# Two transformer blocks on one core: a list scheduler that plans in three passes and ranks ready instructions by deadlines

## The chip, the cores and the metric

The kernel runs on one core of a Trainium2 chip. The metric is the device time of one execution in microseconds (us), from the first to the last instruction and what lies around them; smaller is better. The engines are named as the profile names them: PE (TensorE, the matrix engine; PEld is its weight loading), DVE (VectorE), ACT (ScalarE), POOL (GpSimd) and SP (SyncE, which here only starts DMAs). On-chip memory is SBUF; PE writes its results to PSUM.

## The reference, cut to what matters

Two blocks follow each other, each of two layers and a final norm; 256 tokens of width 1024, fp32. Each layer is a gated feed-forward step of width 2816, a mixing step, and another feed-forward step. The mixing differs: block 1 has neighbourhood attention and gated linear attention (GLA), block 2 has forgetting attention, dilated attention with rotary positions, and HGRN2.

```python
def swiglu(h, w_gate, w_up, w_down):
    return (jax.nn.silu(h @ w_gate) * (h @ w_up)) @ w_down
def hybrid_layer(x, ...):                       # block 1, layer l
    x = x + 0.5 * swiglu(rmsnorm(x, ffn1_norm), ffn1_wg, ffn1_wu, ffn1_wd)
    proj = rmsnorm(x, mix_norm) @ w_in
    na_o = rmsnorm(neighbourhood_attention(na_q, na_k, na_v, na_rpb), na_gain)
    gla_o = rmsnorm(o_fwd + o_bwd, gla_gain) * silu(g_r)   # GLA in both directions
    x = x + concatenate([na_o, gla_o]) @ w_out
    x = x + 0.5 * swiglu(rmsnorm(x, ffn2_norm), ffn2_wg, ffn2_wu, ffn2_wd)
def gla_chunked(q, k, v, g, include_diag):      # one chunk
    b = cumsum(g)
    decay = exp(where(mask, b[:, None] - b[None], -inf))
    a = einsum('td,sd,tsd->ts', q, k, decay)
    ...
def _mixing(h, ...):                            # block 2
    proj = h @ w_in
    oa = _fox_attention(fq, fk, fv, cumsum(log_sigmoid(ff + fox_b)))
    ob = _dilated_attention(_partial_rope(dq), _partial_rope(dk), dv)
    oc = _hgrn2(hq, hf, hi, hg, lb, hgrn_norm)
    return concatenate([oa, ob, oc]) @ w_out
```

## The kernel before, in words

**The matrix products.** Every weight comes from memory as fp32 tiles of 128x1024, 128x704 or 128x768 (`raw`, four buffers, 512 KB each for the largest), started on SP's queue in a fixed sequence. ACT copies a tile to a rounded form (`whi<-raw`), DVE subtracts (`wlo<-raw,whi`), so that a weight is the sum of a high and a low part; activations are kept as a high and a low half side by side (`xhl`, 512 columns). For each 128x128 block of a weight PE multiplies the high part by both halves (128x512) and the low part by the high half (128x256) into the same PSUM bank. This pair is called a block pair below. Banks `acc` and `o` hold features by tokens, `wi` tokens by features. ACT and DVE add the halves (`b<-acc`, `t<-acc,b`) and scale by the norm (`t<-t,rb`, `proj<-t,rb`). A weight tile is wanted by ACT, DVE and PE in the same sequence everywhere.

**The mixing steps.** There are four, called the first to the fourth mixer; the first two belong to block 1. In them the products with `w_in` and `w_out` go on while DVE, ACT and POOL compute the mixing on small tiles. In block 1, DVE scans the gates in two pairs (`C<-g`, four scans in each row), POOL subtracts them (`kq<-C`, function `differences` in `Mixer1.gla`), ACT takes the exponential (`kq<-kq`), DVE multiplies (`kq<-kq,proj`), and PE makes one level of the decay matrix from it (`psA<-kq`, eight levels), which DVE merges (`mg<-mk,psA`). Beside that PE computes attention scores (`psS`), DVE the softmax (`S`, `mx`, `sm`), PE turns them (`psP`). SP moves 16 slabs of values within SBUF in each of these layers (`proj<-proj`, function `slabs`). In block 2 the same chain is called `X<-C`, `X`, `psA<-X`; DVE also turns the dilated heads (`rope<-proj,cs`, `proj<-rope`) before PE transposes them (`psT<-ident,proj`), and computes the forget gate (`fz`, ACT's `ls_e`, `lf`), on which the scores `psS<-tri,lf` rest; ACT takes their exponential (`E`).

**What sets the order.** Nothing is issued while the program is written down: `Program.record` makes an `Op` of each call, with the tiles it uses, its dependencies and an estimated duration (`cost`, and `occ` for PE in `record`, lines 300 to 313). A `Driver` writes the stages down as tasks and jobs; `op.n` is an operation's place in that text. `Program.order` (lines 359 to 452) is a list scheduler: for each of the engines it looks at the operations whose dependencies are placed and whose tile buffers open, and takes the one that could begin first in its model, on a tie the one with the smaller `op.n`:

```python
est = max(op.ready, at, free[e])
k = (est, op.n)
if best[e] is None or k < best[e][0]:
    best[e] = (k, op)
```

The model has one time per engine, a hop of 0.06 between engines, and lets DVE operations with two inputs in SBUF and POOL's exclude each other (`op.port`). `issue` (line 454) then issues all operations in that sequence, so each engine works through a fixed queue in order, and every instruction of the profile has the line 460 (504 in the changed kernel). Buffers of a tile name are handed out in the sequence of the text.

Of the kernel before, what the change touches and what calls it, by code (L numbers as in the profile page):

```python
# [37 lines left out]
def lay_blocks(w, order):  # L38

    b = np.stack([w[f * P:(f + 1) * P, g * P:(g + 1) * P] for g, f in order])  # L40
    return np.ascontiguousarray(b.reshape(-1, 8, P, P).transpose(0, 2, 1, 3)).reshape(-1, P, 8 * P)
# [57 lines left out]
class View:  # L99


    __slots__ = ("tile", "shadow", "chain", "made")

    def __init__(self, tile, shadow, chain=()):
        self.tile, self.shadow, self.chain, self.made = tile, shadow, chain, None
# [80 lines left out]


class Op:
    __slots__ = ("n", "engine", "calls", "occ", "lat", "deps", "after", "wait", "ready", "start", "tiles", "mode", "port")

    def __init__(self, n, engine):
        self.n, self.engine, self.calls, self.occ, self.lat = n, engine, [], 0.0, 0.0
        self.deps, self.after, self.wait, self.ready, self.start = {}, [], 0, 0.0, None
        self.tiles, self.mode, self.port = {}, None, False


class Recorder:
# [7 lines left out]
def free_size(x):  # L205
    n = 1
    for k in x.shape[1:]:
        n *= k
    return n


class Program:
# [61 lines left out]
    def record(self, engine, name, args, kw):  # L274
# [8 lines left out]
        if pe and self.unit is not None:  # L283
            op = self.unit
        else:
            op = Op(len(self.ops), engine)
# [10 lines left out]
        n = max([free_size(x) for x in views] or [1])  # L297
        if pe:
            out, l, r = args[:3]
            if name == "transpose":  # L300
                rows, cols, m = r.shape[0], out.shape[-1], l.shape[0]
                occ = 0.109
                mode = (128, 128)
            else:
                rows, cols, m = l.shape[0], l.shape[-1], free_size(r)
                mode = (128 if rows > 64 else 64, 128 if cols > 64 else 64)
                if r.dtype == F32R:
                    occ = max(m / 2400.0 + (0.02 if m > 256 else 0.0085), 0.109)
                else:
                    occ = 2 * max(m / 1200.0, cols / 1200.0, 0.025) / (2 if mode == (64, 64) else 1) + 0.005  # L310
            if op.mode is not None and op.mode != mode:
                occ += 0.09
            op.mode = mode
            op.occ += occ
            op.lat = self.DRAIN
        else:
            op.occ, op.lat = self.cost(engine, name, args, kw, writes[0] if writes else None, n)
            srcs = [x for x in views if not any(x is w for w in writes) and free_size(x) > 1]
            op.port = name in ("tensor_tensor", "scalar_tensor_tensor") and len(srcs) > 1 and \
                not any(x.tile.bank for x in srcs)  # L320
# [4 lines left out]
        for x in views:  # L325
            t = x.tile
            if op not in t.__dict__.setdefault("seen", set()):
# [3 lines left out]
                if t.index is None:  # L331
                    line = self.tags.setdefault(t.tag, [])
# [24 lines left out]
        t.marks = keep  # L357

    def order(self):
        ops = self.ops  # L360
        for op in ops:
            op.deps.pop(op, None)
            op.wait = len(op.deps)
            for d in op.deps:
                d.after.append(op)
        engines = ("tensor", "scalar", "vector", "gpsimd", "sync")
        free = dict.fromkeys(engines, 0.0)
        avail = {e: [] for e in engines}
# [4 lines left out]
        dma, mode, out = 0.0, None, []  # L373
        port = {"vector": 0.0, "gpsimd": 0.0}

        def opening(op):

            at, need = 0.0, {}
            for t in op.tiles:
                if t.opened:  # L380
                    continue
                s = state[t.tag]
                k = need.get(t.tag, 0)
                if t.index != s[0] + k or s[1] + k >= t.bufs:
                    return None
                if s[0] + k >= t.bufs:
                    at = max(at, s[2][k] + self.HOP)
                need[t.tag] = k + 1
            return at

        best = dict.fromkeys(engines)
        stale = set(engines)
        while len(out) < len(ops):
            for e in stale:
                best[e] = None
                for op in avail[e]:
                    at = opening(op)
                    if at is None:
                        continue
                    est = max(op.ready, at, free[e])  # L400
                    k = (est, op.n)
                    if best[e] is None or k < best[e][0]:
                        best[e] = (k, op)
            stale = set()
            e = min((x for x in engines if best[x]), key=lambda x: best[x][0])
            (start, _), op = best[e]
            avail[e].remove(op)
            stale.add(e)
            if op.port:
                start = max(start, port["gpsimd" if e == "vector" else "vector"])  # L410
# [3 lines left out]
            if e == "tensor":  # L414
                mode = op.mode
            free[e] = start + op.occ + extra
            end = free[e] + op.lat
            if op.calls[0][0] == "dma_start":
# [3 lines left out]
                end = dma + 1.3  # L422
# [17 lines left out]
            for o in op.after:  # L440
# [7 lines left out]
                if not o.wait:  # L448
                    avail[o.engine].append(o)
                    stale.add(o.engine)  # L450
        self.ordered, self.free = out, free
        return out

    def issue(self):
        for op in self.order():
# [1473 lines left out]
```

## Time and profile before

| | |
|---|---|
| time, median of 3 runs | 2033.12 us (2032.52 to 2034.95) |
| the profiled execution, its own time | 2034.24 us |
| its span, first to last instruction | 2032.5 us |
| mean granted PE clock | 0.994 |
| matmuls on PE | 12604 |
| instructions in all | 33794 |

The profile shows one execution. A row of a group names engine, operation, what is written and what is read (buffer numbers left out), how often, and idle time of the engine just before, with the engine and tile that ended it. The chain of waits follows the instruction that ended last back to the first. A stretch's row gives how long each engine was busy within a window of the execution and which share of full clock PE was granted. The feed-forward steps take most of the time; the mixers lie at about 200 to 340, 690 to 840, 1180 to 1340 and 1690 to 1850 us.

### The profile page before, as it was taken

Reading aid. Unit: us, or ns where it says so; the run is one execution under the profiler, and the core shown is the slowest. Engines: PE = TensorE matmul, PEld = TensorE weight load, DVE = VectorE, ACT = ScalarE, POOL = GpSimd, SP = SyncE. Lnnn points to the kernel's source line nnn. Section 1 sums busy time; section 2 is a strip of 40 time slices with the busy share of each in tenths; the row PEclk is TensorE's granted clock in tenths of the full one; section 3 lists DMA queues with packets and bytes.
Section 4 is the critical chain, followed back from the end, with each engine's and each line's share of the span. In section 5 each row is a group of like instructions: output and inputs, shape, how many; then the busy total and the mean of one; then the engine's idle time right before and its main releaser. Section 6 shows DMA issues by size and latency. Waiting matters only on the chain.

```text
span 2032.5 us, 33794 instructions
## 1 busy us (share of the span) xinstructions
PE 1991.9 (98%) x12604; PEld 1745.3 (86%) x12604; DVE 1566.1 (77%) x2405; ACT 1203.5 (59%) x2073; POOL 485.3 (24%) x502
## 2 busy tenths in 40 slices
PE   8999999999999999999999998999999999899997
PEld 7888888888888888888888897888888888788886
DVE  7876888876887698887698678788768867878874
ACT  6654666654665566665566465766546656576653
POOL 3341604331221151221232004122112210412210
PEclk9999999999999999999999999999999999999999
DMA  7655446565555544555566553465555555346652
GB/s 232 196 195 177 151 137 198 192 192 191 181 191 191 161 152 147 192 192 188 176 201 188 193 169 104 128 197 190 190 186 188 187 194 162 122 125 197 191 193 94
DMA packets 104629, 357.35 MB, mean 176 GB/s; under 512 B 13460, under 2 KB 15012, under 8 KB 104464
## 3 DMA queue, kind: packets, MB, share of 16 engines
q1 hardware_dynamic: 101040, 352.20, 54.3%
q0 software_dynamic: 3136, 2.47, 0.5%
q8 instruction: 99, 1.62, 0.3%
q14 instruction: 66, 0.54, 0.1%
q10 hardware_dynamic: 288, 0.52, 0.1%
HBM read 351.98 MB, written 1.51 MB: 174 GB/s over the span
## 4 chain that ended last, share of the span: by engine, by line
PE 84%; DVE 9%; ACT 3%; POOL 2%; issue 1%; DMA 1%; SPq 0%; DVEq 0%; ACTq 0%; POOLq 0%
PE acc L460 51%; PE o L460 27%; DVE wlo L460 3%; PE wi L460 2%; POOL kq L460 1%; ACT whi L460 1%; DVE x L460 1%; PE psO L460 1%; DVE proj L460 1%; DVE xhl L460 1%; DVE X L460 1%; DVE t L460 1%; DVE kq L460 1%; PE psN L460 0%; PE psS L460 0%
## 5 line engine op out<-in xcount | busy, mean ns | idle before, releaser
L460 PE MATMUL acc<-xhl,whi 128*128 128x512 f32 x3328 | 1057.4, 398 | 6.8 <-DVE xhl L460 2.4
L460 DVE TENSOR_TENSOR wlo<-raw,whi 128x1024 fp32r<-128x1024 f32 (+3 forms) x682 | 827.6, 1214 | 187.7 <-ACT whi L460 174.5
L460 ACT ACTIVATE whi<-raw 128x1024 fp32r<-128x1024 f32 (+3 forms) x682 | 704.8, 1034 | 346.3 <-PE o L460 200.1
L460 PEld LDWEIGHTS acc<-xhl,wlo 128*128 128x128 f32 x3328 | 627.1, 188 | 146.9 <-DVE wlo L460 0.4
L460 PE MATMUL acc<-xhl,wlo 128*128 128x256 f32 x3328 | 659.2, 279 | 0.0
L460 PEld LDWEIGHTS acc<-xhl,whi 128*128 128x128 f32 x3328 | 510.4, 189 | 13.8 <-DVE xhl L460 3.7
L460 PE MATMUL o<-hT,whi 128*128 128x512 f32 x1408 | 442.2, 395 | 0.0
L460 POOL TENSOR_TENSOR s<-s,rb 128x256 f32<-128x256 f32 x176 | 215.6, 1225 | 668.0 <-ACT s L460 663.9
L460 ACT ACTIVATE b<-acc 128x256 f32<-128x256 f32 x416 | 158.1, 382 | 332.9 <-PE acc L460 332.5
L460 PEld LDWEIGHTS o<-hT,wlo 128*128 128x128 f32 x1408 | 264.5, 188 | 62.5
L460 DVE TENSOR_TENSOR t<-acc,b 128x256 f32<-128x256 f32 x416 | 174.5, 421 | 139.9 <-ACT b L460 139.8
L460 PE MATMUL o<-hT,wlo 128*128 128x256 f32 x1408 | 276.6, 278 | 0.0
L460 PEld LDWEIGHTS o<-hT,whi 128*128 128x128 f32 x1408 | 214.3, 189 | 0.0
L460 POOL TENSOR_TENSOR sqs<-sqs,sq 128x256 f32<-128x256 f32 x88 | 77.0, 878 | 491.5 <-ACT sq L460 490.9
L460 PE MATMUL wi<-whi,xhl 128*128 128x352 f32 (+2 forms) x448 | 118.8, 335 | 0.8 <-ACT X L460 0.8
L460 DVE SCALAR_TENSOR_TENSOR x<-o,x 128x256 f32<-128x256 f32 x192 | 78.0, 420 | 40.5 <-PE o L460 38.3
L460 DVE TENSOR_TENSOR t<-t,rb 128x256 f32<-128x256 f32 x200 | 86.2, 431 | 5.7
L460 DVE TENSOR_TENSOR t<-t,s 128x256 f32<-128x256 f32 x176 | 75.9, 431 | 18.0 <-POOL s L460 1.2
L460 ACT ACTIVATE s<-t 128x256 f32<-128x256 f32 x176 | 73.4, 417 | 24.7 <-DVE t L460 15.7
L460 DVE TENSOR_TENSOR hT<-t,hT 128x256 fp32r<-128x256 f32 x176 | 84.0, 477 | 0.1
L460 ACT ACTIVATE hT<-t 128x256 fp32r<-128x256 f32 x176 | 73.3, 417 | 18.2 <-DVE t L460 8.3
L460 PEld LDWEIGHTS wi<-whi,xhl 128*128 128x128 f32 x448 | 80.4, 188 | 2.2 <-ACT X L460 1.1
(192 smaller groups left out, 1390.4 us busy)
## 6 DMA issues: line engine op xcount, KB each, us to landing
raw<-in_gu_dram SPq DMA_DIRECT2D x350, 512.0 KB, 3.4
raw<-in_wd_dram SPq DMA_DIRECT2D x176, 512.0 KB, 3.4
raw<-in_win_dram SPq DMA_DIRECT2D x64, 512.0 KB, 3.7
raw<-in_wo_dram SPq DMA_DIRECT2D x32, 512.0 KB, 3.7
raw<-in_win_dram SPq DMA_DIRECT2D x24, 384.0 KB, 3.0
raw<-in_win_dram SPq DMA_DIRECT2D x24, 352.0 KB, 3.0
raw<-in_win_dram SPq DMA_DIRECT2D x8, 388.0 KB, 3.0
proj<-proj SPq DMA_DIRECT2D x32, 64.0 KB, 2.1
```

The costliest lines, as they stand in the source:

```text
L460: getattr(e, name)(*args, **kw)
```

## The change

Operations get a rank, which is `op.n` at first. `order` now runs the same list scheduler (`forward`) three times and keeps the sequence whose modelled end is the earliest. Between two passes `backward` goes through the sequence from its end and gives each operation the latest start at which its dependents, and those that reuse its buffers, are still in time; only PE's operations are also chained one behind the other. That latest start is the operation's rank in the next pass. Among the operations that could begin within 0.001 us of the earliest one, an engine takes the one with the smallest rank, then the smallest `op.n`. Apart from that, PE's modelled cost of small matmuls depends on whether the one before in the same operation has the same shape. No instruction's own work is changed.

```diff
--- before.py
+++ after.py
@@ -186,12 +186,12 @@
 
 
 class Op:
-    __slots__ = ("n", "engine", "calls", "occ", "lat", "deps", "after", "wait", "ready", "start", "tiles", "mode", "port")
+    __slots__ = ("n", "engine", "calls", "occ", "lat", "deps", "after", "wait", "ready", "start", "tiles", "mode", "port", "rank", "late", "left")
 
     def __init__(self, n, engine):
         self.n, self.engine, self.calls, self.occ, self.lat = n, engine, [], 0.0, 0.0
         self.deps, self.after, self.wait, self.ready, self.start = {}, [], 0, 0.0, None
-        self.tiles, self.mode, self.port = {}, None, False
+        self.tiles, self.mode, self.port, self.rank = {}, None, False, n
 
 
 class Recorder:
@@ -304,10 +304,12 @@
             else:
                 rows, cols, m = l.shape[0], l.shape[-1], free_size(r)
                 mode = (128 if rows > 64 else 64, 128 if cols > 64 else 64)
+                side_by_side = op.mode == mode
                 if r.dtype == F32R:
                     occ = max(m / 2400.0 + (0.02 if m > 256 else 0.0085), 0.109)
                 else:
-                    occ = 2 * max(m / 1200.0, cols / 1200.0, 0.025) / (2 if mode == (64, 64) else 1) + 0.005
+                    side = {(128, 128): 1, (128, 64): 2, (64, 128): 2, (64, 64): 4}[mode] if side_by_side else 1
+                    occ = 2 * max(m / 1200.0 / side, cols / 1200.0 if side == 1 else 0.019, 0.019) + 0.005
             if op.mode is not None and op.mode != mode:
                 occ += 0.09
             op.mode = mode
@@ -357,12 +359,54 @@
         t.marks = keep
 
     def order(self):
+
+        for op in self.ops:
+            op.deps.pop(op, None)
+            for d in op.deps:
+                d.after.append(op)
+        for line in self.tags.values():
+            for t in line:
+                t.uses = t.left
+        best = None
+        for k in range(self.PASSES):
+            end, out = self.forward()
+            if best is None or end < best[0]:
+                best = end, out
+            if k < self.PASSES - 1:
+                self.backward(out)
+        self.ordered = best[1]
+        return self.ordered
+
+    PASSES = 3
+
+    def backward(self, out):
+
+        last = max(op.start + op.occ for op in out)
+        front, frees = {}, {}
+        for line in self.tags.values():
+            for t in line:
+                t.needed = last
+        for op in reversed(out):
+            late = front.get(op.engine, last) if op.engine == "tensor" else last
+            for o in op.after:
+                late = min(late, o.rank - (0.0 if o.engine == op.engine else op.lat + self.HOP))
+            for t in op.tiles:
+                late = min(late, t.needed)
+            op.rank = late - op.occ
+            front[op.engine] = op.rank
+            for t in op.tiles:
+
+                if t.index >= t.bufs:
+                    p = self.tags[t.tag][t.index - t.bufs]
+                    p.needed = min(p.needed, op.rank - self.HOP)
+
+    def forward(self):
         ops = self.ops
         for op in ops:
-            op.deps.pop(op, None)
-            op.wait = len(op.deps)
-            for d in op.deps:
-                d.after.append(op)
+            op.wait, op.ready = len(op.deps), 0.0
+        for line in self.tags.values():
+            for t in line:
+                t.left, t.opened, t.end = t.uses, False, 0.0
         engines = ("tensor", "scalar", "vector", "gpsimd", "sync")
         free = dict.fromkeys(engines, 0.0)
         avail = {e: [] for e in engines}
@@ -392,18 +436,18 @@
         stale = set(engines)
         while len(out) < len(ops):
             for e in stale:
-                best[e] = None
+                best[e], can = None, []
                 for op in avail[e]:
                     at = opening(op)
-                    if at is None:
-                        continue
-                    est = max(op.ready, at, free[e])
-                    k = (est, op.n)
-                    if best[e] is None or k < best[e][0]:
-                        best[e] = (k, op)
+                    if at is not None:
+                        can.append((max(op.ready, at, free[e]), op.rank, op.n, op))
+                if can:
+                    first = min(can)[0] + 0.001
+                    k = min((x for x in can if x[0] <= first), key=lambda x: x[1:3])
+                    best[e] = k[:3], k[3]
             stale = set()
             e = min((x for x in engines if best[x]), key=lambda x: best[x][0])
-            (start, _), op = best[e]
+            (start, *_), op = best[e]
             avail[e].remove(op)
             stale.add(e)
             if op.port:
@@ -448,8 +492,8 @@
                 if not o.wait:
                     avail[o.engine].append(o)
                     stale.add(o.engine)
-        self.ordered, self.free = out, free
-        return out
+        self.free = free
+        return max(free.values()), out
 
     def issue(self):
         for op in self.order():
```

The feed-forward steps keep PE's sequence. The first place where the order moves is the first mixer (the second moves alike). On SP's queue, around the 16 slab moves, before and now:

```order
L460 DMA raw<-in_win_dram 128x1024 x4
L460 DMA raw<-in_win_dram 128x704 x4
L460 DMA raw<-in_win_dram 128x1024 x6
L460 DMA proj<-proj 32x512 x16
L460 DMA raw<-in_win_dram 128x1024 x2
L460 DMA raw<-in_win_dram 128x704 x4
```

```order
L504 DMA raw<-in_win_dram 128x1024 x6
L504 DMA proj<-proj 32x512 x2
L504 DMA raw<-in_win_dram 128x1024
L504 DMA proj<-proj 32x512 x5
L504 DMA raw<-in_win_dram 128x1024
L504 DMA proj<-proj 32x512 x7
L504 DMA raw<-in_win_dram 128x704
L504 DMA proj<-proj 32x512 x2
L504 DMA raw<-in_win_dram 128x704 x3
```

The slab moves stood in one piece ahead of the next weights; now three weight tiles go in between them.

On DVE, at the scans of the same mixer (`g` is the gate, `C` its running sum), before and now:

```order
L460 SCALAR_TENSOR_TENSOR g<-psZ,ls_e 128x512
L460 SCALAR_TENSOR_TENSOR C<-g,zero 128x128 x4
L460 SCALAR_TENSOR_TENSOR g<-psZ,ls_e 128x512
L460 TENSOR_TENSOR t<-acc,b 128x256
L460 SCALAR_TENSOR_TENSOR C<-g,zero 128x128 x4
L460 SCALAR_TENSOR_TENSOR proj<-t,rb 128x256
L460 TENSOR_TENSOR wlo<-raw,whi 128x704
L460 TENSOR_TENSOR t<-acc,b 128x256
L460 TENSOR_TENSOR wlo<-raw,whi 128x704
L460 SCALAR_TENSOR_TENSOR proj<-t,rb 128x256
```

```order
L504 SCALAR_TENSOR_TENSOR g<-psZ,ls_e 128x512
L504 SCALAR_TENSOR_TENSOR C<-g,zero 128x128 x4
L504 SCALAR_TENSOR_TENSOR g<-psZ,ls_e 128x512
L504 TENSOR_TENSOR t<-acc,b 128x256
L504 TENSOR_TENSOR wlo<-raw,whi 128x704
L504 SCALAR_TENSOR_TENSOR proj<-t,rb 128x256
L504 TENSOR_TENSOR t<-acc,b 128x256
L504 TENSOR_TENSOR wlo<-raw,whi 128x704
L504 SCALAR_TENSOR_TENSOR proj<-t,rb 128x256
L504 SCALAR_TENSOR_TENSOR C<-g,zero 128x128 x4
```

The second row of scans stood right behind the second gate and one addition; now two weight splits of 704, two scalings and an addition more go ahead of it.

The second place is the third mixer (the fourth moves alike in this part). On PE, where the scores of the forgetting attention follow the last levels of HGRN2, before and now:

```order
L460 MATMUL psA<-X 64x32 x16
L460 MATMUL psA<-X,proj 64x32 x16
L460 MATMUL psS<-tri,lf 128x128 x2
L460 MATMUL psS<-M_11173,identr 128x2x128
L460 MATMUL psS<-tri,lf 128x128 x4
L460 MATMUL psS<-M_11173,identr 128x2x128
L460 MATMUL psS<-tri,lf 128x128 x2
L460 MATMUL psS<-proj 128x256 x4
L460 MATMUL psP<-ident,E 128x128 x8
```

```order
L504 MATMUL psA<-X 64x32 x16
L504 MATMUL psA<-X,proj 64x32 x16
L504 MATMUL wi<-whi,xhl 128x384
L504 MATMUL wi<-wlo,xhl 128x384
L504 MATMUL wi<-whi,xhl 128x384 x2
L504 MATMUL wi<-wlo,xhl 128x384
L504 MATMUL wi<-whi,xhl 128x384 x2
L504 MATMUL wi<-wlo,xhl 128x384
L504 MATMUL wi<-whi,xhl 128x384 x2
L504 MATMUL wi<-wlo,xhl 128x384
L504 MATMUL wi<-whi,xhl 128x384
L504 MATMUL psS<-tri,lf 128x128 x2
```

The scores stood directly behind the levels; now a whole weight tile's products (`wi`, nine rows) come first. Another such tile moved ahead of the levels.

On DVE, at the rotary step of the third mixer, before and now:

```order
L460 TENSOR_TENSOR wlo<-raw,whi 128x1024
L460 SCALAR_TENSOR_TENSOR C<-proj,zero 128x128
L460 COPY_PREDICATED mg<-mk_11171,psA 128x256
L460 TENSOR_TENSOR wlo<-raw,whi 128x1024 x2
L460 TENSOR_SCALAR proj<-wi,rstd 128x384
L460 TENSOR_TENSOR rope<-proj,cs 128x256 x2
L460 TENSOR_TENSOR X<-X,proj 128x16x32
L460 TENSOR_TENSOR proj<-rope 128x2x8x8
```

```order
L504 TENSOR_TENSOR wlo<-raw,whi 128x1024
L504 TENSOR_TENSOR fz<-proj,fb 128x4
L504 TENSOR_TENSOR wlo<-raw,whi 128x1024
L504 TENSOR_SCALAR proj<-wi,rstd 128x384
L504 TENSOR_TENSOR wlo<-raw,whi 128x1024
L504 TENSOR_TENSOR rope<-proj,cs 128x256 x2
L504 TENSOR_TENSOR X<-X,proj 128x16x32
L504 TENSOR_TENSOR proj<-rope 128x2x8x8
```

Two weight splits stood between the last scans and `rope`; now there are three.

## Rows read from the trace of the kernel before

**Rows 1.** Page: busy time of each engine (share of the span), instructions; the chain, by engine.

```profile
PE 1991.9 (98%) x12604; PEld 1745.3 (86%) x12604; DVE 1566.1 (77%) x2405; ACT 1203.5 (59%) x2073; POOL 485.3 (24%) x502
...
PE 84%; DVE 9%; ACT 3%; POOL 2%; issue 1%; DMA 1%; SPq 0%; DVEq 0%; ACTq 0%; POOLq 0%
```

**Rows 2.** Stretches: busy us of each engine (instructions), granted clock, DMA share, GB/s.

```profile
50.00:200.00 150.00, 150.00 (x865) 131.26 (x864) 110.89 (x158) 86.16 (x135) 50.72 (x62) 1.00 0.60 189
225.00:285.00 60.00, 56.55 (x662) 49.67 (x652) 51.13 (x81) 41.02 (x86) 24.36 (x24) 0.97 0.50 157
735.00:795.00 60.00, 55.36 (x525) 49.01 (x524) 48.03 (x87) 40.20 (x88) 8.54 (x14) 0.97 0.42 135
1225.00:1275.00 50.00, 44.44 (x420) 38.82 (x420) 41.62 (x70) 28.82 (x71) 17.90 (x16) 0.93 0.30 88
1735.00:1785.00 50.00, 43.60 (x435) 38.48 (x434) 40.88 (x72) 30.26 (x72) 18.21 (x13) 1.00 0.32 96
```

**Rows 3.** Waits of PE in the whole span: us in total, times, longest us.

```profile
PE psA L460 <- DVE kq L460: 4.2, 4, 2.5
...
PE acc L460 <- ACT ls_e L460: 2.3, 1, 2.3
PE psT L460 <- DVE proj L460: 2.1, 1, 2.1
PE acc L460 <- DVE t L460: 2.1, 3, 1.6
PE psP L460 <- DVE S L460: 2.0, 2, 1.1
PE psS L460 <- DVE mg L460: 1.6, 2, 0.8
PE psA L460 <- ACT E L460: 1.5, 2, 0.8
PE psA L460 <- DVE proj L460: 1.4, 1, 1.4
...
PE psS L460 <- ACT E L460: 1.0, 2, 0.5
PE psS L460 <- DVE proj L460: 0.8, 2, 0.4
PE wi L460 <- ACT X L460: 0.8, 1, 0.8
```

**Rows 4.** Timeline of PE, first mixer: start, us, instructions, [idle before, releaser].

```profile
246.78 0.69 PE L460 MATMUL psA<-kq 64*64 64x64 f32 x32 [1.24 <-DVE kq L460]
```

**Rows 5.** Timeline of ACT, first mixer: a weight's high part, and the exponential behind it.

```profile
243.37 1.06 ACT L460 ACTIVATE whi<-raw 128x1024 fp32r<-128x1024 f32 x1 [4.26 <-DMA raw<-in_win_dram]
244.34 1.04 ACT L460 ACTIVATE kq<-kq 128x1024 f32<-128x1024 f32 x1
```

**Rows 6.** Timeline of POOL, first mixer: the subtractions after the second pair of scans.

```profile
219.93 28.51 POOL L460 TENSOR_TENSOR kq<-C 128x256 f32<-128x256 f32 x26 [0.67 <-DVE C L460]
```

**Rows 7.** Stretches, as rows 2: DVE's work behind the second scans; DVE beside POOL.

```profile
219.77:223.31 3.54, 3.54 (x24) 3.54 (x23) 3.54 (x6) 1.85 (x3) 3.38 (x4) 1.00 0.24 44
...
228.66:246.55 17.89, 16.44 (x203) 13.76 (x201) 16.93 (x20) 12.14 (x20) 17.89 (x16) 1.00 0.61 183
```

**Rows 8.** Instructions that write kq: ns least/median/most, first and last start.

```profile
L460 POOL TENSOR_TENSOR kq<-C x30: 610/800/1692, 216.6 to 247.6; 128x256 f32<-128x256 f32 x30
...
L460 DVE TENSOR_TENSOR kq<-kq,proj x8: 677/1225/1683, 228.7 to 256.1; 128x1024 f32<-128x1024 f32 x7, 128x512 f32<-128x512 f32 x1
```

**Rows 9.** Timeline of DVE, third mixer: a weight split, and a forget gate's wait.

```profile
1234.15 1.75 DVE L460 TENSOR_TENSOR wlo<-raw,whi 128x1024 fp32r<-128x1024 f32 x1
...
1245.99 0.16 DVE L460 SCALAR_TENSOR_TENSOR lf<-fz,ls_e 128x4 f32<-128x4 f32 x1 [3.63 <-ACT ls_e L460]
```

**Rows 10.** DMA issues of the tail: KB each, median us to landing.

```profile
out_dram<-x SPq DMA_DIRECT2D x2, 128.0 KB, 2.2
out_dram<-x SPq DMA_DIRECT2D x1, 256.0 KB, 2.7
```

## The prediction

> **What bounds the kernel now.** I read the page first. PE is busy for 98% of the span and holds 84% of the chain of waits; DVE holds 9%, everything else little [rows 1]. So the kernel is as long as PE's fixed work plus PE's idle time plus what a lowered clock costs. The stretches come next, to see where PE is not full: in a feed-forward stretch of 150 us it is busy for all of them at full clock, and 865 matmuls there make 0.347 us for a block pair of two. In the four mixer stretches it is busy for 56.55 of 60, 55.36 of 60, 44.44 of 50 and 43.60 of 50, and DVE works for 80 to 85% of them [rows 2]. PE's order changes only in the mixers, so everything to be won or lost lies there, apart from the two ends of the program and a norm between the blocks. The third view is the table of PE's waits [rows 3]: the listed ones sum to 19.8 us, about 1% of the time. The fourth thing is the clock: the granted share is 0.97, 0.97, 0.93 and 1.00 in the four mixers [rows 2], that is 1.8, 1.8, 3.5 and 0 us at most (one minus the share, times the stretch). The reader should see a ceiling: some 27 us for a scheduler that makes no mistake.
>
> The sum is made against the profiled execution, 2034.24 us, which lies 1.1 us above the median of the runs.
>
> **First and second mixer: the exponential behind a late weight.** PE waits 4.2 us in four places for `kq` and 0.8 for `proj` in two [rows 3]; the longest in the first mixer is 1.24, at the fifth level [rows 4]. Its cause stands on ACT: the high part of a weight waited 4.26 us for its DMA, and the exponential of `kq` went directly behind it [rows 5]. That DMA was late because SP's queue had 16 slab moves ahead of it. In the new order weights go in between them, and PE's first five levels come 2.8, 2.1, 2.1, 1.4 and 0.7 us later in its own stream (8, 6, 6, 4 and 2 block pairs more ahead of them, 0.347 each). DVE's splits ahead of the fifth level are as many as before, so DVE loses only its idle time. Against it stands the second row of scans, put behind five operations which took 3.54 us [rows 7]. POOL's 26 subtractions start when that scan is done and ran without a pause for 28.51 us, 1.10 each [rows 6]; one more of them is now done ahead, so POOL ends 3.5 - 1.1 = 2.4 us later. For the fifth level that is still in time: by POOL's order 15 subtractions come after the scan for it, which puts its last at about 240, some 4 us before the exponential began [rows 5]. Of the 5.0 us I count 4.0 as gone; the second mixer's longest wait, 2.5, is longer than the 0.7 to 2.1 of its shift. Bounds: 0 and 5.0.
>
> PE's waits for `S`, 2.0 in two layers, go since PE comes to `psP` 2.8 us later; but DVE is as full there as elsewhere, and late weight splits will show in their place. I count 0.5 (bounds 0 and 2.0). The low clock of the first mixer (1.8) I count as gone, since the waits in front of it go; that of the second (1.8) as staying, because part of its 2.5 stays. Together 4.0 + 0.5 + 1.8 = **6.3**.
>
> **Third and fourth mixer, the scores.** PE waits 1.6 for `mg`, 1.5 and 1.0 for `E` and 0.8 for `X` [rows 3], all where dependent blocks stand one behind the other. Now weight tiles stand between them: twelve matmuls of 384 columns, six block pairs' worth, 2.1 us each time, and no wait here is longer than 0.8. The forget gate, for which DVE sat idle 3.63 us at the head of its queue [rows 9], is taken later, when its logarithm is done. Of 4.9 I leave 0.25 per layer: **4.4** gone (bounds 2 and 4.9).
>
> **Third mixer, rope.** One more weight split stands ahead of `rope`; such a split took 1.75 [rows 9]. PE comes to `psT` four block pairs, 1.4 us, later. The wait of 2.1 [rows 3] so grows by 0.35, and the low clock behind it (3.5) stays: **-0.35** (bounds: -0.6 and +5.6, if wait and low clock both go).
>
> **Fourth mixer, rope.** PE's wait of 2.3, shown as for ACT, and 1.4 for `proj` [rows 3] have causes that move: the high parts of the weights now go ahead of the exponentials. But a split is put between the two steps of `rope`, while PE, no longer held, comes to `psT` 2.3 sooner. So the wait mostly moves there, and grows: 2.3 for PE being early and some 1 for the split, of whose 1.75 [rows 9] a part fills idle time. With the 1.4 gone and the 2.3 turned into about 3, I count 1.0 of the 3.7 as won at the best guess. Such a wait is longer than the 2.5 and 2.1 in the second and third mixers, whose stretches show a lowered clock, so I charge 1.8 for it, the price of the second mixer: **-0.8** (bounds -2.5, with the third mixer's 3.5 for the clock, and +3.7).
>
> **The rest.** PE's wait for `t`, 2.1 in three places [rows 3]: the addition that PE waits for goes ahead of others, 0.9 (bounds 0 and 2.1). The last DMA of the program is now one of 128 KB, which lands in 2.2 instead of 2.7 [rows 10]: 0.4. The new order of the first loads I cost at nothing. Together **1.3**. The new price of small matmuls acts through the order alone.
>
> **Sum:** 6.3 + 4.4 - 0.35 - 0.8 + 1.3 = 10.85. 2034.24 - 10.85 = 2023.4, rounded to **2023**.
>
> **The rivals.** *The pair of DVE and POOL is the bound, and the order only moves the waits.* From 228.66 to 246.55 POOL was busy throughout and DVE for 16.93 of 17.89 us [rows 7], and a `kq` multiplication took 1.68 at most against a median of 1.23 [rows 8], so the two hold each other up. If that pair is full, the first two mixers win only the 0.5 and the scores half of theirs, 2.2: 0.5 + 2.2 - 0.35 - 0.8 + 1.3 = 2.85, **2031**. Against it speaks that DVE had idle time to fill, 3.63 in the third mixer [rows 9], and a cause for the first mixer's wait which is a DMA [rows 5]. The Trainium skill, SBUF — State Buffer, section "SBUF: two separate sides", speaks for this rival: it says that a VectorE operation with two inputs in SBUF and a GpSimd operation that reads SBUF exclude each other for the whole instruction. By that rule the stretch would need the sum of both, and it would be no shorter in any order. The trace bears it out in part: five multiplications at 1.23 and 16 subtractions at their median of 0.80 [rows 7, 8] alone make 19.0 us, more than the 17.89 of the stretch, while at the least duration, 0.61, they make 15.9 and leave hardly room for the four weight splits.
>
> *Latest starts leave no slack (slower).* The deadlines come from durations that ignore delays: DVE's 1.68 where 1.23 is usual [rows 8]. The point that decides is whether a chain comes later than PE's block was moved: 0.7 us at the fifth level, 1.4 at `psT`. If POOL's 2.4 us pass on in full to the fifth level, PE waits 1.7 more in each of the first two mixers and nothing there is won: -3.4. At the same time `psT` waits 0.35 more in the third mixer; in the fourth it waits 1.0 more than `acc` did and the clock falls as in the third, -4.5; the scores win nothing. With the 1.3 of the rest that is 6.95 more: **2041**. For it speaks that the scans are moved back by 3.54 [rows 7]; against it, the 4 us of slack which POOL shows before the late exponential [rows 5, 6].
>
> *The clock stays up.* If the waits ahead of the low clock fall short enough, the second mixer's 1.8 and the third's 3.5 go as well, the fourth is not charged and wins its 3.7 instead of 1.0: 10.85 + 1.8 + 3.5 + 1.8 + 2.7 = 20.65, **2014**.
>
> That nothing at all changes can hardly be: the order around every named wait is another.
>
> **How the numbers follow.** My forecast's own range, 2018 to 2028, gets 0.50; the clock rival (2008 to 2018) 0.18; the bound rival (2028 to 2035) 0.20; the slower one 0.12. A measurement of this kernel can tell 0.2% from no change, 4.1 us: faster means below 2029.1, slower above 2037.2. Faster: 0.50 + 0.18 + a quarter of the bound rival's 0.20 = 0.73; within 0.2%: the other 0.15; slower: 0.12. The range 2012 to 2034 leaves out the lowest part of the clock rival, about 0.07, and the slower rival, 0.12.
>
> **What would show it.** Right: the waits of PE for `kq`, `E` and `mg` fall below 2 us in all, ACT no longer stands 4 us for a DMA in the first mixer, the forget gate's wait on DVE is gone, and `psT` is PE's longest wait in both later mixers. Wrong: the first mixers show `kq` waits of 3 us and more behind POOL (the slower rival), or DVE and POOL are both full through the mixers and PE's waits have only changed their names (the bound), or the granted clock is 1.00 in the third mixer (the clock rival). A changed feed-forward stretch would mean that I have missed something altogether.

## The result, and the profile after

The changed kernel takes 2013.24 us (median of 4 runs, 2013.10 to 2014.71) against 2034.03 for the kernel before in the same session; the ratio is 0.990, 95% interval 0.9887 to 0.9912. That is 20.8 us less, 1.0%. The forecast was 2023 with a range of 2012 to 2034: the direction was right and the range held, at its lower edge, but the size was half of what came, and the forecast's own range, 2018 to 2028, was missed. The profiled execution took 2013.10 us with a span of 2011.3.

The page of the kernel after, busy time and chain, as [rows 1]:

```profile
PE 1984.6 (99%) x12604; PEld 1741.6 (87%) x12604; DVE 1566.8 (78%) x2405; ACT 1203.8 (60%) x2072; POOL 498.2 (25%) x502
...
PE 91%; DVE 5%; ACT 1%; issue 1%; DMA 1%; POOL 0%; SPq 0%; DVEq 0%; ACTq 0%
```

PE's share of the chain rose from 84 to 91%. The mixers now, in stretches as [rows 2], which begin some 10 to 20 us earlier in the last two because everything does:

```profile
225.00:285.00 60.00, 58.75 (x659) 52.13 (x659) 53.14 (x86) 41.43 (x88) 28.07 (x27) 1.00 0.50 152
735.00:795.00 60.00, 58.88 (x501) 52.63 (x500) 52.15 (x99) 40.84 (x91) 7.89 (x12) 1.00 0.50 152
1215.00:1265.00 50.00, 47.68 (x472) 42.67 (x472) 45.86 (x78) 32.47 (x83) 17.37 (x15) 1.00 0.35 113
1715.00:1765.00 50.00, 46.91 (x447) 42.01 (x446) 45.29 (x72) 31.76 (x73) 20.10 (x14) 0.97 0.37 117
```

The first three stretches are at full clock; before, they had 0.97, 0.97 and 0.93. The fourth, which was at 1.00, now shows 0.97. PE's waits, four of the eleven rows that are left, as [rows 3]:

```profile
PE psT L504 <- DVE proj L504: 5.4, 2, 3.1
...
PE psP L504 <- DVE sm L504: 1.4, 2, 0.7
PE acc L504 <- DVE t L504: 1.2, 1, 1.2
...
PE psA L504 <- DVE kq L504: 1.0, 3, 0.4
```

The waits for `mg`, `E` and the scores are gone from the list, `psT` leads it. To see where the time came from, the chain of waits has a handle: it contains the same long pieces of PE in both kernels, the second product of a feed-forward step (`o` x352) ahead of each mixer and the first of the next (`acc` x656) behind it. Columns are start and duration. Before:

```profile
135.73 61.31 PE o L460 x352
...
328.06 114.26 PE acc L460 x656
...
627.14 61.31 PE o L460 x352
...
820.00 114.25 PE acc L460 x656
...
1122.14 61.31 PE o L460 x352
...
1334.17 114.26 PE acc L460 x656
...
1633.25 61.31 PE o L460 x352
...
1842.66 114.25 PE acc L460 x656
```

After:

```profile
134.60 61.31 PE o L504 x352
...
322.58 114.26 PE acc L504 x656
...
621.67 61.31 PE o L504 x352
...
809.72 114.26 PE acc L504 x656
...
1111.15 61.31 PE o L504 x352
...
1315.50 114.25 PE acc L504 x656
...
1614.58 61.31 PE o L504 x352
...
1821.19 114.26 PE acc L504 x656
```

From 135.73 to 328.06 are 192.33 us, from 134.60 to 322.58 are 187.98, so the first mixer won 4.35. Done for all, this gives the first row of the table below: 1.1 us at the start of the program, 4.35, 4.81, 7.68 and 2.80 in the four mixers. The stretches between, which hold feed-forward steps and one norm, won 0.7 in all, and the tail lost 0.3. The sum is the 21.2 by which the span fell.

The windows of the four mixers, from the start of `o` to the start of `acc`, also divide what was won. Their sums, before and after (length, then busy time of each engine):

```profile
sum 806.63, PE 785.81 PEld 694.66 DVE 622.56 ACT 477.39 POOL 185.54; mean PE 196.45 PEld 173.67 DVE 155.64 ACT 119.35 POOL 46.38
```

```profile
sum 786.99, PE 778.20 PEld 690.98 DVE 624.10 ACT 478.23 POOL 199.80; mean PE 194.55 PEld 172.75 DVE 156.03 ACT 119.56 POOL 49.95
```

PE's idle time fell from 20.8 to 8.8, by 12.0 us, and its busy time, in which a lowered clock shows, by 7.6.

| won against before, us, from profiled executions | start | mixer 1 | mixer 2 | mixer 3 | mixer 4 | median time, us |
|---|---|---|---|---|---|---|
| the change | 1.13 | 4.35 | 4.81 | 7.68 | 2.80 | 2013.24 |
| prices only | -1.02 | -0.81 | -0.34 | 2.65 | 3.43 | 2032.54 |
| deadlines only | 1.49 | 1.34 | 0.60 | 6.19 | 2.23 | 2023.52 |
| both, DMA queue unranked | 0.50 | 3.38 | 2.25 | 7.60 | 2.72 | 2018.45 |
| prices, DMA queue ranked alone | 1.97 | 0.21 | 0.75 | 2.66 | 0.48 | 2026.96 |
| prices, DVE and DMA queue ranked | 1.97 | 4.61 | 4.86 | 5.13 | 4.21 | 2014.70 |
| the change, psT wait filled | 1.52 | 4.49 | 4.83 | 7.60 | 4.28 | 2011.15 |
| DVE and DMA queue ranked, filled | 1.19 | 4.76 | 4.91 | 8.07 | 4.24 | 2010.03 |

Each row is one execution, which lies up to 2.9 us from the median beside it.

### The profile page after: what moved, and what is told of

It reads as the page before. It is cut to its first block, busy times and chain, and to the rows that moved or that the text cites. A ratio compares the mean times of both kernels' runs of the same rounds, so it can differ in the third digit from the quotient of the medians.

```text
span 2011.3 us, 33848 instructions
## 1 busy us (share of the span) xinstructions
PE 1984.6 (99%) x12604; PEld 1741.6 (87%) x12604; DVE 1566.8 (78%) x2405; ACT 1203.8 (60%) x2072; POOL 498.2 (25%) x502
## 4 chain that ended last, share of the span: by engine, by line
PE 91%; DVE 5%; ACT 1%; issue 1%; DMA 1%; POOL 0%; SPq 0%; DVEq 0%; ACTq 0%
PE acc L504 53%; PE o L504 29%; PE wi L504 4%; DVE wlo L504 2%; PE psA L504 1%; PE psO L504 1%; DVE kq L504 1%; PE psS L504 1%; DVE proj L504 1%; PE psN L504 1%; DVE t L504 1%; ACT whi L504 0%; PE psP L504 0%; DVE S L504 0%; DVE mg L504 0%
## 5 line engine op out<-in xcount | busy, mean ns | idle before, releaser
L504 POOL TENSOR_TENSOR sqs<-sqs,sq 128x256 f32<-128x256 f32 x88 | 87.0, 991 | 472.8 <-ACT sq L504 471.9
```

The lines of the kernel that those rows point to most:

```text
L504: getattr(e, name)(*args, **kw)
```

## The experiments

**One half of the change: the prices.** One pass with the rank equal to the place in the text leaves the new prices of small matmuls alone.

```diff
-    PASSES = 3
+    PASSES = 1
```

> One pass, rank equal to the place in the text, with the new prices of small matmuls: no deadlines at all. Theory (deadlines win the first two mixers through the DMA queue, PE's own sequence wins the scores of the last two): 2025 to 2029 us, the waits for kq and the 4 us of ACT for a weight in the first mixer stay, PE's waits for E and mg in the last two go. Rival (nearly everything comes from PE's new sequence, which the prices make): 2019 us or less, with short waits for kq. Third possibility (the prices do nothing): 2034.

Measured: 2032.54 us, ratio 0.9987 (0.9978 to 0.9996). Neither theory, and nearest to the third possibility: the prices alone move PE's blocks and win 2.2 us. The scores' waits are gone, as expected, worth some 3 us in each of the last two mixers, but the first two mixers, the start and the norm lose most of it again. PE's timeline in the first mixer (start, duration, instructions, idle before) shows why:

```profile
247.74 0.69 PE L504 MATMUL psA<-kq 64*64 64x64 f32 x32 [1.26 <-DVE kq L504]
...
263.61 0.49 PE L504 MATMUL wi<-wlo,xhl 128*128 128x352 f32 x1 [1.49 <-DVE wlo L504]
```

The wait for `kq` at the fifth level is there as before [rows 4], and a second one for a late weight split has come behind it.

**The other half: the deadlines.** Three passes, with the old price.

```diff
-                side_by_side = op.mode == mode
...
-                    side = {(128, 128): 1, (128, 64): 2, (64, 128): 2, (64, 64): 4}[mode] if side_by_side else 1
-                    occ = 2 * max(m / 1200.0 / side, cols / 1200.0 if side == 1 else 0.019, 0.019) + 0.005
+                    occ = 2 * max(m / 1200.0, cols / 1200.0, 0.025) / (2 if mode == (64, 64) else 1) + 0.005
```

> Three passes with deadlines, and the old prices of small matmuls. Theory: the first two mixers win their 9 us, the last two keep most of their waits for E and mg: 2020 to 2025. Rival (PE's new sequence is the cause): 2030 or more, kq waits of 1 us and more stay.

Measured: 2023.52 us, ratio 0.9946 (0.9929 to 0.9963). The total is what the theory said, but not for its reason: the first two mixers win 1.9 us and not 9; most comes from the third. Three of PE's waits:

```profile
PE psP L502 <- DVE S L502: 4.0, 2, 2.0
PE psS L502 <- DVE proj L502: 2.9, 2, 1.4
PE psA L502 <- DVE kq L502: 2.5, 4, 1.0
```

Without the new prices PE's softmax and score blocks stand where they stood, and wait longer than before (4.0 for `S` against 2.0 in [rows 3]). So 2.2 us for one half, 11.2 for the other, 20.8 for both: in the first two mixers (-1.2 and 1.9 alone, 9.2 together) each half needs the other. The third pass has no part in it: the planner's order is the same for every engine after two passes.

**The DMA queue.** Two kernels, one with the ranks everywhere but on SP's queue, one with them there alone.

```diff
     PASSES = 3
+    RANKED = ('tensor', 'scalar', 'vector', 'gpsimd')      # the second kernel: ('sync',)
...
-                        can.append((max(op.ready, at, free[e]), op.rank, op.n, op))
+                        can.append((max(op.ready, at, free[e]), op.rank if e in self.RANKED else op.n, op.n, op))
...
-                    first = min(can)[0] + 0.001
+                    first = min(can)[0] + (0.001 if e in self.RANKED else 0.0)
```

> The whole change, but SP's queue takes the smallest place in the text as before: the 16 slab moves stand in one piece again. Theory: the exponential of kq is stuck behind a late weight again in the first two mixers, which give back most of their 9 us: 2019 to 2022. Rival (the new places of PE's, DVE's and ACT's instructions do it, the DMA queue is beside the point): 2013 to 2015.

> New prices, and deadlines on SP's queue alone; PE, DVE, ACT and POOL go by the place in the text. Theory: 6 to 9 us faster than the kernel with the prices alone, all of it in the first two mixers. Rival: as the prices alone, within 2 us.

Measured: 2018.45 us, ratio 0.992 (0.9905 to 0.9935), and 2026.96, ratio 0.9964 (0.9951 to 0.9977). The wait itself behaves as the theory says. With the queue unranked ACT stands for the weight again, and PE for the fifth level (ACT's and PE's timeline):

```profile
242.27 1.06 ACT L505 ACTIVATE whi<-raw 128x1024 fp32r<-128x1024 f32 x1 [2.80 <-DMA raw<-in_win_dram]
...
247.04 0.69 PE L505 MATMUL psA<-kq 64*64 64x64 f32 x32 [1.65 <-DVE kq L505]
```

PE waits 2.14 in the second mixer. With the queue ranked alone the wait at the fifth level (the second row below) is gone and 0.55 is left at the third, but 1.49 us come back at a weight split, and 1.71 in the second mixer:

```profile
236.19 0.69 PE L505 MATMUL psA<-kq 64*64 64x64 f32 x32 [0.55 <-DVE kq L505]
...
243.41 0.69 PE L505 MATMUL psA<-kq 64*64 64x64 f32 x32
...
259.64 0.66 PE L505 MATMUL wi<-wlo,xhl 128*128 128x352 f32 x1 [1.49 <-DVE wlo L505]
```

So the theory that the queue alone makes the 9 us falls: taking it away costs 3.5 of the 9.2, giving it alone wins 2.1 against the prices alone. The rival falls too, since the median is 5.6 us below that of the prices alone; by the rows of the table 3.0 of them lie at the start. (The execution shown took 2029.89; its fourth mixer was granted 0.93 of full clock over 50 us where the prices alone had 1.00, and won 3 us less.) The queue's order removes one wait, and DVE, which is as full as before, puts another in its place.

**DVE's order with the queue's.** If that is so, DVE's ranks must be the missing part. Against the second of the two kernels:

```diff
-    RANKED = ('sync',)
+    RANKED = ('vector', 'sync')
```

> The new prices, and deadlines on DVE and on SP's queue alone; PE, ACT and POOL go by the place in the text. Theory (in the first two mixers the DMA queue takes away the kq wait and DVE's order keeps it from coming back at wi and psP): 7 us or more of the 9.2 there, 2013 to 2017 in all. Rival (ACT's order is needed too): 4 us or less there, 2019 to 2024 in all.

Measured: 2014.70 us, ratio 0.9902 (0.9887 to 0.9916); the first two mixers win 9.5 us, all that the change wins there. The theory holds, and ranks on ACT, POOL and PE itself add nothing in these mixers (9.2 with them). In the last two this kernel shows something else. PE's timeline and stretches, third mixer first:

```profile
1222.84 1.45 PE L505 MATMUL psT<-ident,proj 128*128 128x128 f32 x8 [2.12 <-DVE proj L505]
```

```profile
1729.80 1.09 PE L505 MATMUL psT<-ident,proj 128*128 128x128 f32 x8 [3.10 <-DVE proj L505]
```

```profile
1215.00:1265.00 50.00, 47.88 (x458) 42.93 (x457) 44.37 (x75) 30.45 (x80) 15.55 (x14) 0.93 0.33 108
1715.00:1765.00 50.00, 46.90 (x467) 41.78 (x466) 46.25 (x75) 31.14 (x74) 21.04 (x14) 1.00 0.36 111
```

A wait of 2.12 us is followed by a lowered clock (0.93 of 50 us, up to 3.5 lost), one of 3.10 is not (1.00). In the changed kernel it is the other way round: 2.3 without, 3.1 with.

**The later second scans.** The forecast's slower rival rested on them. In the first two mixers they go back behind their gate, and nothing else moves.

```diff
-        self.ordered = best[1]
+        out = best[1]
+        for op in [x for x in out if x.calls[0][0] == "tensor_tensor_scan" and x.calls[0][1][1].tile.kw.get("name") == "g"]:
+            out.remove(op)
+            place = {x: i for i, x in enumerate(out)}
+            out.insert(max(place[d] for d in op.deps) + 1, op)
+        self.ordered = out
```

> The changed kernel with one thing undone: in the first two mixers the second scans stand right behind their gate again, everything else in its place. Theory of the forecast (POOL's chain has slack, so the later scan costs nothing): 2012 to 2014.5 us, and the same waits of PE. Rival (POOL ends later and holds up the levels): 2009 to 2011, the kq waits of 0.4 us gone.

Measured: 2014.97 us, ratio 0.9904 (0.9888 to 0.9921); the first two mixers win 4.20 and 4.49, as the change does within 0.3. The total lies 0.5 above the theory's range and far from the rival's: the delay costs nothing that these runs can show. POOL's timeline of the changed kernel shows what it gave up:

```profile
215.51 3.81 POOL L504 TENSOR_TENSOR kq<-C 128x256 f32<-128x256 f32 x5 [14.40 <-DVE C L504]
221.77 28.55 POOL L504 TENSOR_TENSOR kq<-C 128x256 f32<-128x256 f32 x25 [2.45 <-DVE C L504]
```

Five subtractions are done ahead, 25 follow without a pause and end at 250.32, where they ended at 248.44 [rows 6]; counted from the start of the mixer, which comes 1.1 us sooner, that is 3.0 later. The fifth level does not notice:

```profile
240.40 1.05 ACT L504 ACTIVATE whi<-raw 128x1024 fp32r<-128x1024 f32 x1
241.35 1.05 ACT L504 ACTIVATE kq<-kq 128x1024 f32<-128x1024 f32 x1
```

The fifth level's exponential starts at 241.35 behind a weight that is there, where it started at 244.34 behind one that came late [rows 5]. Behind it ACT does stand for POOL, 0.62, 1.86 and 0.64 us, but no wait of PE above 0.45 comes of it.

**The clock.** Eight matmuls of 512 columns fill the waits ahead of `psT` in the last two mixers; their results are overwritten.

```diff
...
+            first = op.calls[0][1][0] if op.calls[0][0] == "transpose" else None
+            if first is not None and first.tile.kw.get("name") == "psT" and first.tile not in self.filled:
+                if len(self.filled) % 2 == 0:
+                    for _ in range(8):
+                        e.matmul(first.tile.real()[:, :512], self.fill[0].real(), self.fill[1].real(), start=True, stop=True)
+                self.filled.append(first.tile)
...
```

> The changed kernel with eight matmuls of 512 columns, whose results are overwritten, ahead of the first psT transposes of the last two mixers; some 1.8 us of work inside waits of 2.3 and 3.1. Theory (the clock falls because PE idles, and costs about 1.7 in the fourth mixer): low clock gone there, 2011 to 2012. Rival (the fall does not hang on that wait, or the added matmuls delay the transposes): 2013 to 2016.

Measured: 2011.15 us, ratio 0.9882 (0.9867 to 0.9897). The stretches of the last two mixers:

```profile
1215.00:1265.00 50.00, 49.47 (x480) 44.03 (x479) 45.60 (x77) 32.86 (x84) 16.54 (x14) 1.00 0.36 111
1715.00:1765.00 50.00, 48.73 (x476) 43.06 (x475) 46.21 (x74) 31.27 (x74) 18.91 (x14) 1.00 0.37 117
```

The theory holds: the fourth mixer is back at 1.00 and wins 4.28 instead of 2.80, the third stays as it was. 1.5 us is what the lowered clock cost there by these two executions, and `psT` is not delayed.

**The rotary step first.** The other way to shorten that wait is to have its cause done sooner.

```diff
...
+                    hot = [x for x in can if x[3].first and x[0] <= first + 0.3]    # x[3].first: writes or reads rope
+                    if hot:
+                        k = min(hot, key=lambda x: x[:3])
```

> The changed kernel, with the rotary step of the last two mixers taken by DVE as soon as it is ready within 0.3 us, ahead of the weight split and the X multiplications. Theory (order: the split and the multiplications ahead of it make the psT waits of 2.3 and 3.1): those waits fall below 0.5 each and the low clock in the fourth mixer goes: 2006 to 2009. Rival (DVE and POOL together are full there, so the wait moves to the late split and PE waits for it at acc): 2011 to 2015, psT short, acc or wi waiting for wlo by 2 us and more.

Measured: 2012.21 us, ratio 0.9888 (0.9874 to 0.9903), 1 us below the changed kernel. The time is the rival's, but not its sign: PE no longer waits for `psT`, and waits not for a late split but for the multiplications that were put off and for ACT's `b`:

```profile
PE psA L509 <- DVE X L509: 2.7, 2, 2.3
...
PE psA L509 <- ACT b L509: 1.6, 1, 1.6
```

The fourth mixer's stretch stays at 0.97, now behind a wait of 2.3 for `X`. So the wait moved, as the rival says, and the clock fell behind the new one.

**POOL beside DVE.** So what fills DVE there? In this kernel the subtractions `X<-C` of the last two mixers are replaced by memsets.

```diff
+                if op.engine == "gpsimd" and name == "tensor_tensor" and op.calls[0][1][0].tile.kw.get("name") == "X":
+                    e.memset(args[0], 0.0)
+                    continue
```

> The changed kernel with POOL's subtractions of the running sums in the last two mixers (X<-C) left out: each is a memset of the same tile, in the same place of the order, which reads nothing. Theory (POOL's reads stretch DVE's operations, rope from 0.4 to 1.2 and the splits from 1.2 to 2.0, and that makes the psT waits): both waits below 0.5, no low clock in the fourth mixer, 2005 to 2009 us. Rival (the extra split alone makes them): waits of 1.5 and more stay, 2011 to 2014.

Measured: 2004.86 us, ratio 0.9848 (0.9834 to 0.9863). The instructions of DVE that write for the rotary step, in nanoseconds (least, median, most), in the changed kernel and here:

```profile
L504 DVE TENSOR_TENSOR rope<-proj,cs x4: 1271/1292/1323, 1216.8 to 1721.6; 128x256 f32<-128x256 f32 x4
L504 DVE TENSOR_TENSOR proj<-rope x4: 1154/1187/1203, 1220.7 to 1727.5; 128x128 f32<-128x128 f32 x4
```

```profile
L507 DVE TENSOR_TENSOR rope<-proj,cs x4: 418/418/419, 1214.6 to 1715.3; 128x256 f32<-128x256 f32 x4
L507 DVE TENSOR_TENSOR proj<-rope x4: 282/283/289, 1215.9 to 1717.6; 128x128 f32<-128x128 f32 x4
```

And the two stretches here, with PE busy for all of them:

```profile
1215.00:1265.00 50.00, 50.00 (x509) 44.84 (x507) 38.94 (x80) 33.77 (x85) 3.27 (x7) 1.00 0.32 105
1715.00:1765.00 50.00, 50.00 (x498) 44.74 (x496) 38.77 (x80) 34.56 (x86) 2.62 (x5) 1.00 0.33 111
```

The four steps of a rotary chain take 1.4 us instead of 5.0, no `psT` wait is left, and the last two mixers win 10.2 and 7.6. The theory holds, with one limit: the memsets are shorter, wait for nothing and ran earlier, so this shows what POOL's subtractions cost DVE, not whether reading is the part that hurts.

**A faster version.** The best ranks and the fill together; the second kernel has ranks on ACT as well.

> The new prices, deadlines on DVE and SP's queue alone, and the eight matmuls ahead of psT. Theory (the low clock in the third mixer, 6.8 us at half, came from that wait, and the fill takes it away as it did in the fourth): 3 us less than without the fill, 2009 to 2012. Rival (the clock falls elsewhere, or the fill delays the transposes): 2013 to 2016.

> As before, with deadlines on ACT too; PE and POOL go by the place in the text. Theory (PE's own deadlines add nothing, its place in the text is as good): 2008 to 2012, not slower than the changed kernel with the fill. Rival (PE's deadlines matter in the last two mixers): 2013 to 2017, new waits of PE there.

Measured: 2010.03 us, ratio 0.9873 (0.9856 to 0.9889), and 2012.65, ratio 0.9886 (0.9871 to 0.9900). With ranks on DVE and SP's queue and the fill, the third mixer wins 8.07 instead of the 5.13 without the fill:

```profile
1215.00:1265.00 50.00, 49.69 (x485) 44.58 (x484) 44.35 (x77) 33.31 (x84) 16.84 (x14) 1.00 0.35 110
1715.00:1765.00 50.00, 48.76 (x475) 43.16 (x474) 45.49 (x78) 32.15 (x82) 18.67 (x13) 1.00 0.37 116
```

Both stretches are at full clock, as the theory said. This kernel beats the one before by 1.3% and the changed one by 3 us in the medians, although the two intervals touch at 0.9887 to 0.9889. Ranks on ACT as well make it slower, by 2.6 us in the medians; the execution kept wins 8.3 us in the first two mixers instead of 9.7. Its theory missed by 0.65 us, and the rival's new waits in the last two mixers are not there: a cause of the 2.6 is not shown.

## Why the forecast was right, and why it was half

**Where the time lies.** Right: the feed-forward stretches did not change by 0.02 us, and everything came from the mixers, the start and the norm. All four signs of being right came: 1.0 us of waits for `kq`, `E` and `mg` is left, ACT no longer stands for a DMA in the first mixer, the forget gate's `lf` waits for nothing on DVE, and `psT` is PE's longest wait in both later mixers. But one sign of being wrong came too, full clock in the third mixer. Over the four mixers the forecast's terms make 9.6 us of waits and nothing net for the clock; measured are 12.0 of idle time and 7.6 of busy time. Most of the missing half is in PE's busy time.

**First and second mixer, 6.3 forecast, 9.2 measured.** Of the 5.0 of waits for `kq` and `proj`, 1.0 is left, so 4.0 went, as said. Of the 2.0 at `psP` 1.4 is left, so 0.6 went for a forecast of 0.5; what is left waits for the softmax (`sm`) and not for a late split. The low clock is the mis-sized term: I let the second mixer's 1.8 stay, because I expected part of its wait of 2.5 to stay, and both mixers are now at 1.00. The cause I named, a weight stuck behind 16 slab moves, is shown for the one wait: ACT stands 2.8 to 5.6 us for such a weight in each of these mixers of every kernel whose queue is unranked, and 0.6 us at most ahead of an exponential of `kq` in every kernel whose queue is ranked. It is not the cause of the whole gain: I wrote that late splits would show in the place of the wait, and charged 1.5 for it, without seeing that DVE's deadlines are what prevents that. Nor did I separate the two halves of the change: PE's later blocks come from the prices, and are worth nothing without DVE's new order.

**The scores, 4.4 forecast.** None of the waits for `mg`, `E` and `X`, 4.9 before, is left in the list. Prices alone already remove those for `mg` and `E`.

**Third mixer, rope, -0.35 forecast.** The wait grew from 2.15 to 2.32, by half of what I had said. But the low clock behind it, which I let stay, did not come: up to 3.5 us, the largest single error (2.9 is what it cost in the kernel with ranks on DVE and SP's queue, by its rows without and with the fill). With the second mixer's 1.8 the two make 5.3 of the 10 us by which the sum was short. Of the rest I can assign 0.5 to the scores, and some 2 us to waits of 0.5 us and less that I had not listed (for `wlo` at `wi`, for `X` and `mg` at `psA`, for `whi` at `psP`); they are gone too. About 2 us are busy time of PE beyond what the granted clock explains, and stay open.

**Fourth mixer, rope, -0.8 forecast.** Right in kind and nearly in size: the wait of 2.3 moved to `psT` and grew to 3.1, where I had said about 3, and a lowered clock followed, 0.97 of 50 us, or 1.5, where I had charged 1.8.

**The rest, 1.3 forecast.** 1.13 at the start, 0.7 at the norm and -0.3 in the tail make 1.6. The start, costed at nothing, gave the most of these; PE's wait for POOL there fell from 2.7 to 0.9. The wait for `t` fell by 0.9, as said. The tail's 0.4 was wrong in sign, since the DMAs of 128 KB took 2.7 there where they had taken 2.2 [rows 10].

**The rivals.** The clock rival, 2014 with a chance of 0.18, is what happened in the first three mixers; in the fourth its condition was not met. That its number is within 1 us is luck: the 4.5 us that it gives the fourth mixer on top did not come, and about as much that no term of the forecast had came in their place. The slower rival's mechanism is shown to cost nothing: POOL ended 1.9 us later and its slack covered that. The bound rival was wrong for the first two mixers, where a better order took PE's idle time from 8.5 to 3.4 us, and right in kind for the rotary step: there the order that was tried won 1 us, and taking POOL's work away 8.4. For that place the Trainium skill, SBUF — State Buffer, section "SBUF: two separate sides", has a VectorE instruction with two SBUF inputs and a GpSimd instruction that reads SBUF shut each other out for the whole instruction. The runs agree with it, since 0.42 us became 1.29 and 0.28 became 1.19 beside subtractions, but they do not show that the reading is what decides.

## What to carry to other kernels

A wait that is removed from a full engine's consumer can come back at the next thing that engine makes, as here, unless that engine's own order changes with it; so rank the full engine by what the bound engine needs, and correct the bound engine's prices at the same time, because in the first two mixers here neither half was worth much alone. Look at every DMA queue for small transfers ahead of large ones that an in-order engine will stand and wait for. A low clock behind a wait should enter a forecast as a chance, not as a fixed part of the wait.

## What was not expected of the hardware

The clock does not follow from the length of the wait. Where it falls, it falls to half, the lower of its two levels (1.2 of 2.4 GHz); in the kernel before, behind the 2.15 us of the third mixer, a window of 5 us shows it (columns as [rows 2]):

```profile
1235.00:1240.00 5.00, 5.00 (x43) 4.37 (x42) 5.00 (x10) 1.19 (x2) 2.70 (x3) 0.50 0.29 82
```

After 2.15 us (before) and 2.12 us (ranks on DVE and SP's queue) at `psT` of the third mixer, the granted clock of the stretch was 0.93; after 2.32 in the changed kernel it was 1.00. In the fourth mixer 3.09 gave 0.97 and 3.10 gave 1.00. Executions of one kernel differ as well: the ten of the prices alone go from 2029.3 us at a mean granted clock of 0.996 to 2033.9 at 0.991. So a difference of 2 or 3 us between two such kernels can be the clock's luck. But it need not be luck alone. In the kept execution of all five unfilled kernels with POOL's subtractions in which PE goes by the ranks, the third mixer's stretch is at 1.00 and the fourth's at 0.97; in all four in which PE goes by the place in the text the third is at 0.93, and the fourth at 1.00 but for one. With one execution of each, whether PE's order decides is not shown. Filling the wait with overwritten matmuls took the lowered stretch away in both kernels that were kept with and without it (the fourth mixer of the one, the third of the other).
